# Planning around shared PSUM banks, a new order for the last triple, and last stores on two queues

## The chip, the cores and the metric

The kernel runs on one core of a Trainium2 chip. The metric is the device time of one execution in microseconds (us). Each kernel is run several times and the median counts. One further execution is recorded by the hardware profiler, and all rows and traces come from that one.

The core's engines have short names in the profile: PE is TensorE's matmul, PEld its weight load, DVE is VectorE, ACT is ScalarE, POOL is GpSimd, and SP is SyncE. A "q" behind a name (SPq) means that engine's instruction sequencer, which also issues DMAs.

## The reference

```python
# x [16, 512, 1024], w1 [1024, 768], w2 [1024, 768], all float32
y1 = np.matmul(x, w1)
y2 = np.matmul(x, w2)
return (np.tanh(y1) * y2).astype(np.float32)
```

## The kernel before

**Tiling.** The 16 x 512 rows of x are 64 row tiles of 128 rows. The columns of the two weights are put into three blocks of 512: `a` (the first 512 of w1), `b` (the first 512 of w2) and `g` (the last 256 of w1 and the last 256 of w2). K = 1024 is split into two halves of 512. All matmuls are float16 with float32 sums in PSUM, whose eight banks hold 128 x 512 each.

**Head and triples.** The first four row tiles (the head) are multiplied plainly: eight matmuls for each block. The other 60 row tiles are done in 20 triples, numbered 0 to 19. A triple is three row tiles of two halves each, times three column blocks of two halves each. Done plainly it would take 18 block products; a fast scheme needs 15, p0 to p14. Each product multiplies a sum of x blocks (`A_SUMS`, made for every triple by VectorE at L417, written S10, S21, ...) with a sum of weight blocks (`B_SUMS`, made once). A product is four matmuls of 128x128 by 128x512 (L442) and accumulates in a PSUM bank called a chain, c0 to c10.

**Between the products** stand the steps of `C_OPS`: `copy` (ScalarE, L446, bank to SBUF), `seed` (ScalarE, L446, bank to a second bank in which a later product goes on accumulating), `add` (VectorE, L452, a bank plus or minus a copy). At the end each row tile gets `t` and `th` (tanh on ScalarE, L455, 512 and 256 columns) and `m` and `mh` (the multiplication on VectorE, L460), and its output is stored (`store`, L423). A step is written with its triple: add60.19 is the step add60 of triple 19. The steps that matter below are these:

- add60 reads the bank of p0 (and a copy) and seeds the bank of p4; t0 also reads the bank of p0.
- copy60 reads the result of p4; add52 needs copy60 and the result of p5; seed16 copies add52's result and so starts the bank of p2; p3 goes on in add52's bank after seed16 has read it.
- add4 and th1 both read the result of p3; th0 reads add4's result; t1 reads add8's result, and add8 needs copy60. m1 multiplies with the result of p2, mh1 with that of p3, mh0 with add4's.
- add64 is needed by p12, add312 by p9, add2 by p5.
- The triple's third row tile has t2 and m2 (result of p13), th2 and mh2 (result of p14).

**Fillers.** Row tile 3 of the head leaves out its `g` block. Its 16 matmuls of 256 columns (L426, written m3y0k and m3y1k) are set between the products of the last triple. Then follow thg3 (tanh, L429) and mug3 (multiplication, L433).

**The order of the work.** All steps are handed to a `Planner`, which runs a small model of the engines and fixes each engine's program order. PE's order of products is written out by hand (`PE_ORDER`, and `LAST_ORDER` at L71 for triple 19) and kept strictly. For the other engines, `run` (L135) looks at each engine's ready steps: `pick` (L125) prefers, among those that can start within 0.02 us of the earliest, the one with the nearest due time. Of the engines, the one whose pick starts first goes next. A step may start when what it needs is done. The model knows nothing of two engines reading one bank at the same time: it plans t0.19 and add60.19 for the same moment. The framework that builds the program then adds the waits that keep two engines off one bank, in the planned order.

**Stores.** SyncE issues all stores. In the last triple each row tile is stored in two parts: st610, st620, st630 are the 512-column parts of row tiles 61 to 63 (multiplied by m0, m1, m2), st611, st621, st631 the 256-column parts (mh0, mh1, mh2). st3M is the last 256 columns of row tile 3, behind mug3.

**Beside it** ScalarE runs one abs instruction per row tile (D4 to D63, L386), whose sums decide at the very end, through a flag read by all engines and an `If`, whether a general path must run. For this input it does not. At the join behind the `If`, SyncE waits on several semaphores and then on all of them before the program ends.

Of the kernel before, what the change touches and what calls it, by code (L numbers as in the profile page):

```python
# [67 lines left out]

PE_ORDER = "7 0+ 13+ 6 10 4+ 5+ 9 12 1 14 3+ 2+ 11 8"
FIRST_ORDER = "7 1 10 6 12 9 11 8 14"  # L70
LAST_ORDER = "0 14 4 5 13 3 2"  # L71


class Planner:
# [9 lines left out]
    def op(self, name, engines, due, needs, fn, *args, behind=(), issued=(), chains=(), xfer=0.0, latency=None, seeds=False,  # L84
           lands=None, hold=0.0):
        assert name not in self.ops, name
        self.ops[name] = dict(engines=engines, due=due, needs=[n for n in needs if n], behind=[n for n in behind if n], issued=[n for n in issued if n], fn=fn, args=args,
                              chains=chains, xfer=xfer, latency=latency, seeds=seeds, lands=lands, hold=hold)
        for c in chains:
            self.chains.setdefault(c, {"left": 0, "bank": None, "end": 0.0})["left"] += 1  # L90

    def backward(self, margin):
        users = {n: [] for n in self.ops}
# [41 lines left out]
    def run(self):  # L135
        free = {"pe": 0.0, "act": 0.0, "dve": 0.0, "pool": 0.0, "sp": 0.0}
        bandwidth = 1.25
        left = {n: len(o["needs"] + o["behind"] + o["issued"]) for n, o in self.ops.items()}
        ready_at, end, engine_of, start_of = {n: o["hold"] for n, o in self.ops.items()}, {}, {}, {}
        ready = {e: [] for e in free}  # L140

        def release(n):
            for e in self.ops[n]["engines"]:
                ready[e].append(n)

        for n in self.ops:
            if not left[n]:
                release(n)
        position, lag = 0, 0.0
        strict = set(self.strict)  # L150
        while len(end) < len(self.ops):
            best = None
            for e, names in ready.items():
                options = []
                for n in names:
                    if n in strict and n != self.strict[position]:
                        continue
                    o = self.ops[n]
                    s = max(free[e], ready_at[n])
                    new = [c for c in o["chains"] if self.chains[c]["bank"] is None]  # L160
                    if new:
                        fit = self.fitting(o)
                        if not fit:
                            continue
                        s = max(s, min(fit)[0])
                    options.append((s, o["due"], n))
                if not options:
                    continue
                s, due, n = self.pick(e, options, lag)
                if best is None or s < best[0]:  # L170
                    best = s, e, n
            assert best, ("stuck", [(n, self.ops[n]["needs"]) for n in self.strict[position:position + 3]])
            s, e, n = best
            o = self.ops[n]
            for c in o["chains"]:
                if self.chains[c]["bank"] is None:
                    entry = min(self.fitting(o), key=lambda b: (b[0] > s, b[1] not in self.partial, b[0]))
                    self.bank_free.remove(entry)
                    self.chains[c]["bank"] = entry[1]
                    if not o["seeds"]:  # L180
                        (self.partial.add if c[0] in ("T", "f") else self.partial.discard)(entry[1])
            f = s + o["engines"][e]
            free[e] = f
            if o["lands"]:
                done = o["lands"]
                bandwidth = max(bandwidth, done - 1.6)
            elif o["xfer"]:
                bandwidth = max(bandwidth, f) + o["xfer"]
                done = bandwidth + (o["latency"] or self.LATENCY["cast" if e == "pool" else "sp"])
            else:  # L190
                done = f
            end[n], engine_of[n], start_of[n] = done, e, s
            for k in o["engines"]:
                ready[k].remove(n)
            if n in strict:
                position += 1
                lag = s - o["due"]
            for c in o["chains"]:
                chain = self.chains[c]
                chain["end"] = max(chain["end"], done + self.LATENCY[e])  # L200
                chain["left"] -= 1
                if not chain["left"]:
                    self.bank_free.append((chain["end"], chain["bank"]))
            for u in self.next.get(n, ()):
                ready_at[u] = max(ready_at[u], f)
                left[u] -= 1
                if not left[u]:
                    release(u)
            for u in self.users[n]:
                same = e in ("act", "dve", "pe") and e in self.ops[u]["engines"]  # L210
                slack = 1.0 if n in self.ops[u]["behind"] and self.ops[u]["xfer"] else 0.0
                ready_at[u] = max(ready_at[u], done + slack + (0.06 if same else 0.05 if o["xfer"] or o["lands"] else self.LATENCY[e]))
                left[u] -= 1
                if not left[u]:
                    release(u)
        self.end, self.engine_of, self.start_of = end, engine_of, start_of
        return sorted(self.ops, key=lambda n: start_of[n])
# [22 lines left out]
def kernel(  # L240
# [7 lines left out]
    nc = tc.nc  # L248
    P = 128
    B, M, K = x.shape  # L250
    _, N = w1.shape
# [6 lines left out]
    TRIPLES = (MT - HEAD) // 3  # L258
# [10 lines left out]
    of = out.flatten_outer_dims().rearrange("(mt p) n -> mt p n", p=P)  # L269
# [41 lines left out]
    pin = tc.keep_in_program_order  # L311
    engine = {"dve": nc.vector, "act": nc.scalar, "pool": nc.gpsimd, "sp": nc.sync}
    plan = Planner(8)
    op = plan.op
# [104 lines left out]
    def out_tile(mt):  # L419
        return o_bufs[mt if mt < HEAD else HEAD + (mt - HEAD) % O_BUFS]  # L420

    def store(e, mt, lo=0, n=N):
        pin(nc.sync.dma_start(of[mt][:, lo:lo + n], out_tile(mt)[:, lo:lo + n]))  # L423

    def mm(e, chain, mt, k, rhs, first):
        pin(nc.tensor.matmul(bank(chain)[:, :rhs.shape[-1]], xt(mt)[:, k, :], rhs, start=first, stop=k == KO - 1, skip_group_check=True))  # L426
# [88 lines left out]
    for n, what in enumerate(on_sp):  # L515
# [3 lines left out]
        else:  # L519
            s, k = what[0], int(what[1])  # L520
# [54 lines left out]
    outs = {mt: [] for mt in range(MT)}  # L575
# [15 lines left out]
    for n, s in enumerate("agb"):  # L591
        for mt in range(HEAD):
            if (s, mt) == ("g", HEAD - 1):
                continue
            due, behind = (lambda n: landed[slices["agb".index(s) * KO + n]] + 0.8 + 0.02 * mt), [FILL[mt]] if s == "b" and mt in FILL else []
            finals(mt, s, due(KO - 1) + (5.0, 3.0, 7.0)["agb".index(s)], plain(mt, s, due, behind))

    mt = HEAD - 1
    ends = {}
    for t, after in enumerate(("p0", "p2")):  # L600
        chain = ("f", f"y{t}")
        for n, k in enumerate(range(KO)):
            op(f"m{mt}y{t}{k}", {"pe": MM / 2}, 1e4 * (1 + t) + n, [f"cg{k}", f"e{mt}{k // KH}"], mm, chain, mt, k,
               wh[:, k, F + t * G:F + t * G + G], n == 0, behind=[f"m{mt}y{t}0" if n else f"{after}.{TRIPLES - 1}"], chains=[chain])
        ends[t] = [f"m{mt}y{t}{k}" for k in range(KO)]
        xt_readers[mt] += ends[t]
# [43 lines left out]
    LAST = 2.0  # L650
    TIME = {"t": 0.5, "m": 0.6, "th": 0.28, "mh": 0.33, "add": 0.6, "copy": 0.5, "seed": 0.5, "p": SLOT}
    soonest, until = {}, {}
# [4 lines left out]
    for i in range(TRIPLES):  # L657
# [10 lines left out]
        for o in C_OPS:  # L668
            name, kind, needs = o[:3]
            needs = [f"{n}.{i}" for n in needs]  # L670
            chains = sorted({(i, p) for p in o[3:6] if isinstance(p, str) and p[0] == "c"})
# [14 lines left out]
                continue  # L686
            r = o[3]
            mt = HEAD + 3 * i + r
            due = soonest[i, name] + LAST
            if kind in ("t", "th"):  # L690
                lo, n = (0, F) if kind == "t" else (F, G)
                op(f"{name}.{i}", {"act": 0.5 if n == F else 0.285}, due, needs, c_tanh, i, r, o[4], lo, n, o[5],
                   behind=reuse_out(mt), chains=chains)
            else:
                lo, n, at = (0, F, 0) if kind == "m" else (F, G, G)
                op(f"{name}.{i}", {"dve": 0.6 if n == F else 0.335}, due + 1, needs, c_mul, i, r, o[4], lo, n, at, chains=chains)
                outs[mt].insert(0 if kind == "m" else 1, f"{name}.{i}")
    for mt in range(MT):
        i = (mt - HEAD) // 3 if mt >= HEAD else -1
        if mt < HEAD:  # L700
            n = F if mt == HEAD - 1 else N
            op(f"st{mt}", {"sp": 0.05}, 1e3, outs[mt][:1] if mt == HEAD - 1 else outs[mt], store, mt, 0, n, behind=[f"p12.{4 + mt}"], xfer=1.0)
            if n < N:
                op(f"st{mt}M", {"sp": 0.05}, 2e4, outs[mt][1:], store, mt, n, N - n, xfer=0.4)
            continue
        late = [f"{('p0', 'p4', 'p12')[(mt - HEAD) % 3]}.{i + 1}"] if i < TRIPLES - 2 else []
        if i == TRIPLES - 1:
            for a, lo, n in ((0, 0, F), (1, F, G)):
                part = outs[mt][a:a + 1]
                op(f"st{mt}{a}", {"sp": 0.05}, 2e4, part, store, mt, lo, n, xfer=0.4)  # L710
        else:
            op(f"st{mt}", {"sp": 0.05}, slot_of[max(i, 0), "p2"] + 12, outs[mt], store, mt, behind=late, xfer=1.0)
    for mt in range(BY_PE, MT):
# [9 lines left out]
    for mt in range(HEAD, MT):  # L723
        i, r = divmod(mt - HEAD, 3)
# [16 lines left out]
    for n in sorted(soon, key=lambda n: plan.start_of[n]):  # L741
        o = plan.ops[n]
# [3 lines left out]
    for n in order:  # L746
        if n not in soon:
            o = plan.ops[n]
# [102 lines left out]
```

## Time and profile before

| what | us |
|---|---|
| three runs | 302.2, 301.41, 301.7 |
| median | 301.7 |
| the profiled execution | 301.63 |
| its span, first to last instruction | 299.9 |
| PE busy in it | 291.0 |
| DVE busy | 255.9 |
| ACT busy | 224.9 |

The granted TensorE clock of the profiled execution is 0.999 of full speed. The span is what the trace shows; the profiled execution took 1.73 us more than it. A busy PE means that matmuls are in flight, not that they follow each other at the best rate; idle time of an engine counts only where the last work waits for it. The chain of waits follows the work that ended last back from the end, and so names what each stretch of the span waited for. In rows of the timeline, `[0.52 <-ACT o L455]` means that the engine stood idle for 0.52 us and was released by ScalarE's instruction of line 455 that writes `o`.

### The profile page before, as it was taken

To read this page: it belongs to the slowest core of one execution; us is meant where nothing else is said; L and a number is where in the kernel's file an instruction comes from. 1 tells how busy PE (TensorE), PEld (TensorE's weight loads), DVE (VectorE), ACT (ScalarE), POOL (GpSimd) and SP (SyncE) were. 2 spreads that over 40 slices of the span, in tenths; PEclk is the share of its full clock that TensorE was granted. 3 is DMA by queue.
4 is the path that set the end of the run, shared out by engine and by line. 5 is a ranking of instruction groups with operands and counts; after the bars stand their busy time and mean duration, and the time that the engine had idled before them with its cause. 6 is when DMAs were issued, how large, how long until landed. Compare 5 with 4: busy or idle time off the path is not lost.

```text
span 299.9 us, 4690 instructions
## 1 busy us (share of the span) xinstructions
PE 291.0 (97%) x1385; PEld 133.8 (45%) x1385; DVE 255.9 (85%) x538; ACT 224.9 (75%) x451; POOL 49.8 (17%) x128
## 2 busy tenths in 40 slices
PE   8989999999999999999999999999999999999994
PEld 5434444444444444444444444444444444444442
DVE  1669989989889898988988898898988989897874
ACT  2587997597978879798786988759687776867542
POOL 0064042121102102211011211112022110000000
PEclk9999999999999999999999999999999999999999
DMA  6999999999999999999999999999999999141233
GB/s 231 380 291 200 178 184 169 176 223 237 244 168 187 229 173 301 272 254 259 161 243 243 300 204 258 221 245 252 190 224 251 145 224 296 56 160 52 106 143 142
DMA packets 84283, 63.51 MB, mean 212 GB/s; under 512 B 62752, under 2 KB 66336, under 8 KB 84256
## 3 DMA queue, kind: packets, MB, share of 16 engines
q1 hardware_dynamic: 73888, 45.36, 61.9%
q0 software_dynamic: 9792, 16.78, 37.6%
q10 hardware_dynamic: 576, 1.05, 1.0%
q8 instruction: 11, 0.18, 0.2%
q14 instruction: 16, 0.13, 0.2%
HBM read 39.85 MB, written 25.17 MB: 217 GB/s over the span
## 4 chain that ended last, share of the span: by engine, by line
PE 85%; DMA 7%; DVE 4%; issue 1%; ACT 1%; ACTq 0%; SPq 0%; POOL 0%; DVEq 0%
PE bank L442 82%; DMA arena<-in_w_dram 4%; PE bank L426 3%; DMA wh<-in_w_dram 2%; DMA xT<-xh 1%; DVE bank L452 1%; DVE early_x L417 1%; DVE o L460 1%; PE bank L376 0%; DVE arena L452 0%; ACTq L353 0%; DVE b L408 0%; ACT o L455 0%; ACT wh L362 0%; SPq L350 0%
## 5 line engine op out<-in xcount | busy, mean ns | idle before, releaser
L442 PE MATMUL bank<-b,early_x 128*128 128x512 f16 x640 | 148.2, 379 | 0.8 <-DVE bank L452 0.4
L442 PEld LDWEIGHTS <-early_x 128*128 128x128 f16 x800 | 78.2, 98 | 95.7 <-issue 1.7
L446 ACT ACTIVATE arena<-bank 128x512 f32<-128x512 f32 x100 | 59.0, 597 | 38.8 <-PE bank L442 37.9
L452 DVE TENSOR_TENSOR bank<-bank,arena 128x512 f32<-128x512 f32 x100 | 69.3, 694 | 19.0 <-ACT arena L446 13.6
L460 DVE TENSOR_TENSOR o<-o,bank 128x512 f32<-128x512 f32 (+1 forms) x120 | 61.1, 548 | 5.2 <-ACT o L455 3.5
L386 ACT ACTIVATE junk<-xh 128x1024 f16<-128x1024 f16 x60 | 63.1, 1051 | 0.1
L442 PEld LDWEIGHTS <-xT 128*128 128x128 f16 x400 | 38.9, 98 | 47.9 <-issue 1.2
L442 PE MATMUL bank<-b,xT 128*128 128x512 f16 x240 | 58.3, 379 | 0.0
L358 POOL DMA_DIRECT2D xh<-in_x_dram x60 | 31.8, 530 | 77.6 <-ACT junk L386 60.2
L442 PE MATMUL bank<-wh,xT 128*128 128x512 f16 x160 | 41.1, 379 | 0.8 <-DVE o L460 0.5
L455 ACT ACTIVATE o<-bank 128x256 f32<-128x256 f32 (+1 forms) x80 | 32.9, 436 | 11.2 <-DVE bank L452 7.7
L442 PE MATMUL bank<-wh,early_x 128*128 128x512 f16 x160 | 41.1, 379 | 0.0
L417 DVE TENSOR_TENSOR early_x<-early_x,xT 128x512 f16<-128x512 f16 x80 | 32.2, 418 | 1.3 <-DMA xT<-xh 0.6
L455 ACT ACTIVATE o<-arena 128x512 f32<-128x512 f32 x40 | 25.0, 624 | 6.8 <-DVE arena L452 6.7
L479 POOL CAST held<-xT 128x1 f32<-128x1 f16 x53 | 12.6, 239 | 103.7 <-DMA xT<-xh 103.7
L446 ACT ACTIVATE bank<-bank 128x512 f32<-128x512 f32 x40 | 21.5, 570 | 1.6 <-DVE bank L452 1.1
L426 PE MATMUL bank<-wh,xT 128*128 128x512 f16 x72 | 19.1, 379 | 1.4 <-DVE wh L364 0.7
L417 DVE TENSOR_TENSOR early_x<-xT,early_x 128x512 f16<-128x512 f16 x40 | 16.7, 418 | 0.0
L417 DVE TENSOR_TENSOR early_x<-xT,xT 128x512 f16<-128x512 f16 x40 | 16.6, 416 | 0.0
L452 DVE TENSOR_TENSOR bank<-arena,bank 128x512 f32<-128x512 f32 x20 | 13.9, 695 | 2.4 <-PE bank L442 0.5
L452 DVE TENSOR_TENSOR arena<-arena,bank 128x512 f32<-128x512 f32 x20 | 13.5, 677 | 0.3 <-issue 0.3
L452 DVE TENSOR_TENSOR arena<-bank,arena 128x512 f32<-128x512 f32 x20 | 13.8, 688 | 0.0
(47 smaller groups left out, 136.0 us busy)
## 6 DMA issues: line engine op xcount, KB each, us to landing
out_dram<-o SPq DMA_DIRECT2D x60, 384.0 KB, 5.5
xh<-in_x_dram POOLq DMA_DIRECT2D x60, 256.0 KB, 6.3
arena<-in_w_dram SPq DMA_DIRECT2D x12, 256.0 KB, 5.7
early_x<-in_x_dram SPq DMA_DIRECT2D x8, 256.0 KB, 5.4
arena<-in_w_dram ACTq DMA_DIRECT2D x4, 256.0 KB, 6.1
wh<-in_w_dram POOLq DMA_DIRECT2D x8, 128.0 KB, 4.9
out_dram<-o SPq DMA_DIRECT2D x4, 256.0 KB, 2.7
xT<-xh SPq DMA_TRANSPOSE x57, 6.1
```

The costliest lines, as they stand in the source:

```text
L358: pin(nc.gpsimd.dma_start(xh(mt), xf[mt]))
L386: pin(nc.scalar.activation(junk[:, :src.shape[-1]], src, ACT.Abs, scale=scale, accum_out=sums[:, column:column + 1]))
L417: pin(engine[e].tensor_tensor(x_operand(i, v), x_operand(i, a), x_operand(i, b), OP[how]))
L426: pin(nc.tensor.matmul(bank(chain)[:, :rhs.shape[-1]], xt(mt)[:, k, :], rhs, start=first, stop=k == KO - 1, skip_group_check=True))
L442: pin(nc.tensor.matmul(place(i, dst), x_operand(i, a)[:, k, :], w_rhs(b, k), start=begins and k == 0, stop=k == KH - 1, skip_group_check=T ...
L446: pin(nc.scalar.activation(place(i, dst), place(i, src), ACT.Copy, scale=float(sign)))
L452: pin(nc.vector.tensor_tensor(place(i, dst), a, b, ALU.add if signs == (1, 1) else ALU.subtract))
L455: pin(nc.scalar.activation(out_tile(HEAD + 3 * i + r)[:, lo:lo + n], place(i, src)[:, :n], ACT.Tanh, scale=float(sign)))
L460: pin(nc.vector.tensor_tensor(o, o, place(i, src)[:, at:at + n], ALU.mult))
L479: pin(nc.gpsimd.tensor_copy(held, xt(mt)[:, 0, :1]))
```

## The change

The planner now notes for each chain when ScalarE and when VectorE last finished on it. A step of one of them may only be planned after the other's last one on the same chain, plus that engine's latency. Of two engines whose picks start at the same time, the one with the nearer due time goes first.

`LAST_ORDER` changes, and both groups of fillers may start once p14.19 is planned (before: the first group after p0.19, the second after p2.19). Their matmuls keep a late due time and fill what the products leave. th1.19 is due 1.0 us later.

The last stores (st3M, and all parts of triple 19) may be issued by SyncE or by ScalarE, at 0.4 us in the plan.

```diff
-LAST_ORDER = "0 14 4 5 13 3 2"
+LAST_ORDER = "0 5 4 13 14 3 2"
+FILLERS = "p14", "p14"
...
-            self.chains.setdefault(c, {"left": 0, "bank": None, "end": 0.0})["left"] += 1
+            self.chains.setdefault(c, {"left": 0, "bank": None, "end": 0.0, "act": 0.0, "dve": 0.0})["left"] += 1
...
+                    if e in ("act", "dve"):
+                        other = "dve" if e == "act" else "act"
+                        s = max([s] + [self.chains[c][other] + self.LATENCY[other] for c in o["chains"]])
                     options.append((s, o["due"], n))
...
-                if best is None or s < best[0]:
-                    best = s, e, n
+                if best is None or (s, due) < best[0]:
+                    best = (s, due), e, n
...
-            s, e, n = best
+            (s, _), e, n = best
...
                 chain["end"] = max(chain["end"], done + self.LATENCY[e])
+                if e in ("act", "dve"):
+                    chain[e] = done
...
     def store(e, mt, lo=0, n=N):
-        pin(nc.sync.dma_start(of[mt][:, lo:lo + n], out_tile(mt)[:, lo:lo + n]))
+        pin(engine[e].dma_start(of[mt][:, lo:lo + n], out_tile(mt)[:, lo:lo + n]))
...
-    for t, after in enumerate(("p0", "p2")):
+    for t, after in enumerate(FILLERS):
...
-            due = soonest[i, name] + LAST
+            due = soonest[i, name] + LAST + (1.0 if (i, name) == (TRIPLES - 1, "th1") else 0.0)
...
-                op(f"st{mt}M", {"sp": 0.05}, 2e4, outs[mt][1:], store, mt, n, N - n, xfer=0.4)
+                op(f"st{mt}M", {"sp": 0.4, "act": 0.4}, 2e4, outs[mt][1:], store, mt, n, N - n, xfer=0.4)
...
-                op(f"st{mt}{a}", {"sp": 0.05}, 2e4, part, store, mt, lo, n, xfer=0.4)
+                op(f"st{mt}{a}", {"sp": 0.4, "act": 0.4}, 2e4, part, store, mt, lo, n, xfer=0.4)
```

In the program that this builds, PE's order in triple 19 is p0, p5, p4, p13, p14, four fillers, p3, p2, twelve fillers; before it was p0, p14, one filler, p4, p5, p13, seven fillers, p3, p2, eight fillers. On ScalarE st631 stands between t1.19 and th0.19, and st621 and st3M behind thg3. SyncE keeps st610, st630, st620 and st611, in this order. VectorE's last steps are add4, m1, mh1, mh0, mug3; before they were add4, mh1, m1, mh0, mug3. ScalarE's order there is th0, th1, thg3; before it was thg3, th1, th0.

## The prediction

> **What bounds the kernel now.** I read the page first. Its first part says which engine is full.
>
> ```profile
> span 299.9 us, 4690 instructions
> ...
> PE 291.0 (97%) x1385; PEld 133.8 (45%) x1385; DVE 255.9 (85%) x538; ACT 224.9 (75%) x451; POOL 49.8 (17%) x128
> ```
>
> PE is busy 97% of the span, so only time in which PE waits, or time after its last matmul, can be won. Next the chain of waits in order of time (start, length, what) shows where that is.
>
> ```profile
> 54.43 223.86 PE bank L442 x1036
> ...
> 278.31 9.53 PE bank L442 x44
> ...
> 287.86 0.61 ACT o L455
> ...
> 288.49 0.71 DVE bank L452
> ...
> 289.24 2.75 PE bank L442 x12
> ...
> 293.67 0.71 DVE bank L452
> ...
> 294.40 0.39 ACT o L455
> ...
> 296.09 0.41 DVE o L433
> ```
>
> From 54.43 to 287.8 the chain is PE alone: 223.86 / 1036 = 0.216 us per 512-wide matmul, so a product of four takes 0.86. Then it leaves PE twice: for t0.19 and add60.19 (287.86 to 289.20), and after p3.19 for add4.19, th1.19 and the last multiplications. The timeline of the first place:
>
> ```profile
> 286.80 1.03 PE L442 MATMUL bank<-b,xT 128*128 128x512 f16 x4
> ...
> 287.86 0.60 ACT L455 ACTIVATE o<-bank 128x512 f32<-128x512 f32 x1
> ...
> 288.49 0.70 DVE L452 TENSOR_TENSOR bank<-bank,arena 128x512 f32<-128x512 f32 x1 [0.52 <-ACT o L455]
> ...
> 289.24 0.59 PE L442 MATMUL bank<-b,early_x 128*128 128x512 f16 x2 [0.45 <-DVE bank L452]
> 289.25 0.31 PEld L442 LDWEIGHTS <-early_x 128*128 128x128 f16 x2 [0.62 <-issue]
> ```
>
> p0.19 starts at 286.80 and its readers at 287.86, so a product's result is there 1.06 after its first matmul. t0.19 (ScalarE) and add60.19 (VectorE) both only read its bank, yet add60.19 starts 0.03 after t0.19 ends: the two are kept apart on a bank. p4.19 needs add60.19. Without a wait it would have followed p14.19 (287.66 + 0.86) and one filler (0.11), at 288.63; it starts at 289.24, so 0.61 is lost. Last, the end, from the SyncE rows of the store line and of the join after the last `If`:
>
> ```profile
> L423 SPq DMA_DIRECT2D out_dram<-o x9: 332/333/1670, 286.2 to 296.8; - x9
> ...
> L753 SPq EVENT_SEMAPHORE  x5: 17/17/17, 297.3 to 297.6; - x5
> ...
> L846 SPq EVENT_SEMAPHORE  x14: 17/28/28, 298.2 to 299.8; - x14
> ```
>
> The last multiplication ends at 296.50, the last store is issued at 296.76 and lands 1.9 later, at 298.63. Behind the issue SyncE runs five waits 0.08 apart from 297.31, then the final waits; the one for the last store passes at 298.73, 0.06 after its neighbour like the rest, so no wait holds it. The end is SyncE's own work behind its last issue.
>
> **The change, part by part**, on the clock of the trace before.
>
> *The loop.* In the built order, PE's first difference is behind p0.19, and POOL has none. VectorE and ScalarE exchange neighbours in triples 0, 1, 4, 9 and 18: D22 ahead of t0.4, D37 ahead of t0.9, add8 ahead of add52, and the like. Some banks swap numbers, which costs nothing. SyncE gets one transpose (T28) ahead of two stores, whose out tiles are reused nine row tiles later. What covers this is the lead of the feeds: seed16 ends 1.0 before p3 in nearly every triple, and 0.47 in triple 9, 0.33 in triple 18; add64.5 ends 1.62 before p12.5, add64.10 1.03 before p12.10. add52 goes back by one VectorE step (0.60), but seed16 starts 0.6 to 0.7 after add52 in triples 4 and 9, behind ScalarE work. t0.4 goes back by an abs instruction (1.05 plus 0.2 for its sum); add60 no longer waits for it, and the m0 behind it leaves add64 inside the lead. In triple 18 copy60 moves ahead of t2.19 and starts some 1.0 earlier than its 281.09, which pays for add8 ahead of add52. Without the cover a place would cost 0.1 to 0.6; I take nothing, and the head (before 54) stays: its stall at 53.56 hangs on mh1.0, which does not move.
>
> *Last triple, order of PE.* p0, p5, p4, p13, p14, four fillers, p3, p2, twelve fillers. p5.19 takes p14's place at 287.66; it needs add2.19, which ends at 287.66 (0.05 at worst). add60.19 now stands ahead of t0.19: 287.87 to 288.57. p4.19 starts at 288.62 against 289.24: 0.62 won. t0.19 goes behind (288.60 to 289.20), and only m0.19 waits for it. p13 and p14 (0.86 each) and four fillers (0.44) bring PE to 291.64. Meanwhile: p4's result 289.68, copy60.19 0.60, add52.19 0.70, seed16.19 0.60, with 0.03 to 0.05 at each handover: p3.19 at 291.69, against 292.60. Here 0.91 is won, because add52.19 stood until 291.24 for p5.19, which is now done early.
>
> *The end of compute.* p2.19 starts at 292.55, its result is there at 293.61, and m1.19 now goes directly behind add4.19: 293.61 to 294.31 (before: 295.15 to 295.84). Before, VectorE stood 0.45 for th1.19, which had waited for add4.19 on the same bank; now m1.19 fills that time. PE's last filler ends at 293.41 + 12 x 0.11 + 0.16 = 294.9, so mug3 runs from 294.93 to 295.34 against 296.50: 1.16 won.
>
> *The stores.* st631, st621 and st3M move to ScalarE's queue. Behind st631 stand th0.19, th1.19 and thg3: it waits for mh2.19 (done about 292.6) and takes 0.33 to 0.46 (the store rows, and the ScalarE loads of the first microseconds). th0.19 waits for add4.19 until 293.4 anyway, so this is covered by some 0.3; uncovered it would move thg3 and mug3 by as much. The other two have no compute behind them. Before, SyncE's four last issues queued, so that st3M began 0.26 after mug3 instead of the usual 0.03: 0.23 is what a second queue can give. The Trainium skill says the same in "DMA: Bandwidth & Descriptors", section "Issuing engines are not separate DMA queues": starting transfers on several engines saves only the sequencer's time. By it alone the move would be worth those 0.23 and no landing would change.
>
> *What is late next.* SyncE's last issue (st611, behind mh0.19) ends near 295.4, so its own tail would start 1.7 earlier. But in the built program the second of the five waits counts the store of m1.19 (st620). That is issued at 294.34 and, with the 2.0 of the equal store before, lands at 296.36; the wait passed at 297.39 before. So everything behind it moves by 1.0. st3M, issued at 295.37 and landing after 1.9, is there at 297.3; its final wait comes 1.34 behind the second one, at 297.7, and is not held.
>
> **Sum.** 1.0 off the span: 298.9. The profiled execution took 301.63, 1.73 more than its span, so 300.6; it lies 0.07 under the median of 301.7. Forecast 300.7.
>
> **Rivals.**
> 1. *More is won.* If SyncE's join wait is not held (a store that lands in 1.7, as the smaller ones do, gives 0.3 of it), the last store sets the end: landing at 297.3 against 298.7 for its wait, 1.4 won, 300.3. For it: landings of 1.7 occur. Against it: the 512-wide halves took 2.0.
> 2. *The cover is lost.* The chain p4, copy60, add52, seed16 ends at 291.64, exactly when PE arrives with only four fillers instead of seven before p3. One VectorE or ScalarE instruction in its way (0.4 to 0.6) passes straight to m1 and st620: 0.4 to 0.6 won, 301.1 to 301.3. For it: no slack. Against it: m0.19 ends near 289.9, 0.4 before add52 is wanted.
> 3. *ScalarE's queue lands late: slower.* The only rows of that queue are the first loads:
>
> ```profile
> arena<-in_w_dram ACTq DMA_DIRECT2D x4, 256.0 KB, 6.1
> ...
> out_dram<-o SPq DMA_DIRECT2D x4, 128.0 KB, 1.9
> ```
>
> If st3M took 6.1 from 295.37, it would land at 301.5 and the end come 1.2 later, at 302.6: 2.7 lost, 304.4. It decides from a landing of 3.4, where the end is as before. Against it: SyncE's equal loads in the same crowd took 5.7, and at the end the DMA engines are nearly idle; but one SyncE issue there took 1.67 instead of 0.33. By the rule above (Trainium skill, "DMA: Bandwidth & Descriptors", "Issuing engines are not separate DMA queues") this rival has nothing for it, since the queues share their engines.
>
> That the change does not do what it says is excluded for the order (the built program shows it), not for its worth.
>
> **How the numbers follow.** A measurement of this kernel tells 0.3% (0.9 us) from no change. Forecast 0.50, rival 1 0.17, rival 2 0.23, rival 3 0.10. The forecast lies just past that bound, so I put two thirds of it (0.33) to faster; with rival 1 that makes 0.50. Same: 0.17 of the forecast, rival 2's 0.23, and 0.02 of rival 3: 0.42. Slower: 0.08. The range runs from rival 1 less 0.2 (300.1) to rival 2 plus 0.4 (301.7), about the scatter of the three runs (301.41 to 302.2).
>
> **What would show it.** Right: p4.19 starts within 0.15 of the end of p5.19, PE idles under 0.1 before p3.19, VectorE has no wait for ScalarE behind add4.19, mug3 ends 8.5 after p0.19 starts, against 9.70, and SyncE's second join wait stands for a landing. Wrong: a new idle piece of PE between 54 and 287, a wait of PE on ScalarE before p3.19, or a final wait held by a ScalarE store.

## The result, and the profile after

The changed kernel takes 300.03 us (median of 22 runs) against 301.44 for the kernel before (22 runs beside it). The ratio is 0.9958, with a 95% interval of 0.9945 to 0.9970: faster by 0.4%, just past the 0.3% that can be told. Applied to the 301.7 from which the prediction started, that is 300.4 (300.0 to 300.8); 300.7 was forecast. The profiled execution took 299.76, its span is 297.9.

The page's first part shows the same picture as before, one percent fuller:

```profile
span 297.9 us, 4694 instructions
...
PE 290.5 (98%) x1385; PEld 134.1 (45%) x1385; DVE 256.0 (86%) x538; ACT 224.8 (75%) x451; POOL 51.6 (17%) x128
```

The chain of waits on this page holds only mug3 (0.42 us), so it answers nothing. A table by stage does. Below it is first for the kernel before, then for the changed one. The cuts are the starts of p7.1, p7.2 and p0.19; columns are the stretch, its length, then busy time and instructions of each engine, the clock, the DMA share and GB/s.

```profile
core 0: us, PE busy (x) PEld busy (x) DVE busy (x) ACT busy (x) POOL busy (x), PEclk, DMA share, GB/s
0.00:40.77 40.77, 37.37 (x205) 18.62 (x205) 27.92 (x63) 28.17 (x52) 10.68 (x26) 1.00 1.05 250
40.77:54.43 13.66, 13.16 (x60) 5.81 (x61) 13.49 (x31) 11.54 (x25) 4.01 (x11) 1.00 1.11 161
54.43:286.80 232.37, 232.37 (x1078) 105.20 (x1079) 207.50 (x433) 180.60 (x366) 35.12 (x92) 1.00 1.03 211
286.80:299.86 13.06, 8.12 (x45) 4.20 (x43) 6.95 (x14) 4.60 (x10) 0.00 (x0) 0.98 0.44 163
```

```profile
0.00:40.31 40.31, 36.95 (x204) 18.79 (x205) 28.07 (x64) 27.74 (x52) 10.52 (x26) 1.00 1.06 255
40.31:53.48 13.17, 13.12 (x61) 5.81 (x60) 13.17 (x30) 11.65 (x25) 5.91 (x13) 1.00 1.03 192
53.48:285.74 232.26, 232.26 (x1078) 105.31 (x1078) 207.70 (x434) 181.03 (x367) 35.21 (x91) 1.00 0.99 209
285.74:297.89 12.15, 8.14 (x45) 4.20 (x43) 7.05 (x13) 4.43 (x10) 0.00 (x0) 0.93 0.47 175
```

The last stage is 0.91 shorter: that is the forecast term (1.0 was forecast). But the second stage is 0.49 shorter, the loop 0.11, and the first 0.46. The forecast had nothing for these three. In the second stage VectorE is busy 13.49 of 13.66 us before and 13.17 of 13.17 after: it has no idle time at all there.

The first place of triple 19, as the timeline of the changed kernel shows it (start, length, engine and operation, idle time before it and its releaser):

```profile
286.60 2.05 PE L448 MATMUL bank<-b,early_x 128*128 128x512 f16 x8
...
286.87 0.70 DVE L458 TENSOR_TENSOR bank<-bank,arena 128x512 f32<-128x512 f32 x1
287.61 0.60 ACT L461 ACTIVATE o<-bank 128x512 f32<-128x512 f32 x1 [1.07 <-DVE bank L458]
287.63 1.39 PEld L448 LDWEIGHTS <-early_x 128*128 128x128 f16 x7 [0.28 <-issue]
288.24 0.69 DVE L466 TENSOR_TENSOR o<-o,bank 128x512 f32<-128x512 f32 x1 [0.67 <-ACT o L461]
```

add60.19 runs first. ScalarE is idle for 1.07 ahead of t0.19, and the last 0.7 of it is add60.19. p4.19 starts at 287.63, behind p5.19 with 0.16 of idle time inside the row of eight matmuls (before: 0.61). The end of the work:

```profile
290.21 0.60 PE L432 MATMUL bank<-wh,xT_kept 128*128 128x256 f16 x4
...
290.68 1.89 PE L448 MATMUL bank<-b,xT 128*128 128x512 f16 x8
...
291.74 0.69 DVE L458 TENSOR_TENSOR bank<-arena,bank 128x512 f32<-128x512 f32 x1 [0.21 <-PE bank L448]
...
292.66 1.35 DVE L466 TENSOR_TENSOR o<-o,bank 128x512 f32<-128x512 f32 x3 [0.23 <-PE bank L448]
...
293.71 1.06 ACTq L429 DMA_DIRECT2D out_dram<-o  x2
293.99 0.42 DVE L439 TENSOR_TENSOR o<-o,bank 128x256 f32<-128x256 f32 x1
```

p3.19 starts 0.14 after the last of the four fillers, where fillers follow each other by 0.11: 0.03 is lost. VectorE waits for PE only, no longer for ScalarE. Last the stores and the join: the rows of the two lines (count, shortest, median and longest in ns, first and last start), and from SyncE's waits the one behind the join.

```profile
L429 ACTq DMA_DIRECT2D out_dram<-o x3: 338/350/362, 291.6 to 294.4; - x3
...
L759 SPq EVENT_SEMAPHORE  x5: 17/17/17, 294.5 to 295.7; - x5
...
L852 SPq EVENT_SEMAPHORE  x14: 17/28/28, 296.2 to 297.8; - x14
```

```profile
SPq L429 <- DVE o L466: 4.5, 3, 2.2
SPq L759 <- SPq L759: 0.9, 1, 0.9
```

The five join waits spread from 294.5 to 295.7, because the second stands 0.9. It counts m1.19's store st620, issued at 293.38, which landed at 295.41; the wait passed at 295.43.

### The profile page after: what moved, and what is told of

It is laid out like the page before. It is cut to its first block, busy times and chain, and to the rows that moved or that the text cites. A ratio compares the mean times of both kernels' runs of the same rounds, so it can differ in the third digit from the quotient of the medians.

```text
span 297.9 us, 4694 instructions
## 1 busy us (share of the span) xinstructions
PE 290.5 (98%) x1385; PEld 134.1 (45%) x1385; DVE 256.0 (86%) x538; ACT 224.8 (75%) x451; POOL 51.6 (17%) x128
## 5 line engine op out<-in xcount | busy, mean ns | idle before, releaser
L485 POOL CAST held<-xT 128x1 f32<-128x1 f16 x53 | 14.9, 282 | 35.1 <-DMA xT<-xh 35.1
```

The lines of the kernel that those rows point to most:

```text
L485: pin(nc.gpsimd.tensor_copy(held, xt(mt)[:, 0, :1]))
```

## The experiments

All lengths below are from the profiles, cut as in the table above; "ratio" is against the runs of the kernel before on the same chip.

| kernel | ratio (95%) | to p7.1 | p7.1 to p7.2 | p7.2 to p0.19 | p0.19 to end |
|---|---|---|---|---|---|
| before | | 40.77 | 13.66 | 232.37 | 13.06 |
| changed | 0.9958 (0.9945 to 0.9970) | 40.31 | 13.17 | 232.26 | 12.15 |
| changed, again (e11) | 0.9967 (0.9945 to 0.9990) | 40.73 | 13.41 | 232.26 | 12.14 |
| e1 order only | 0.9991 (0.9979 to 1.0002) | 40.45 | 13.67 | 232.38 | 12.73 |
| e2 rule only | 0.9960 (0.9945 to 0.9975) | 42.58 | 13.41 | 232.26 | 12.53 |
| e3 stores only | 0.9999 (0.9990 to 1.0008) | 40.36 | 13.66 | 232.38 | 13.08 |
| e4 order and rule | 0.9970 (0.9948 to 0.9993) | 40.96 | 13.42 | 232.25 | 12.14 |
| e5 order and stores | 0.9993 (0.9977 to 1.0009) | 40.27 | 13.66 | 232.36 | 12.72 |
| e6 rule and stores | 0.9973 (0.9961 to 0.9985) | 40.46 | 13.40 | 232.25 | 12.56 |
| e7 whole store | 0.9959 (0.9945 to 0.9972) | 40.60 | 13.34 | 232.26 | 12.31 |
| e8 order, one exchange | 0.9960 (0.9945 to 0.9975) | 40.59 | 13.67 | 232.37 | 12.18 |
| e9 one exchange, triple 0 | 0.9997 (0.9988 to 1.0006) | 40.76 | 13.42 | 232.38 | 13.05 |
| e10 changed, mh1.0 earlier | 0.9936 (0.9922 to 0.9951) | 40.55 | 12.96 | 232.26 | 12.13 |
| e12 before, mh1.0 earlier | 0.9984 (0.9971 to 0.9998) | 41.15 | 13.01 | 232.38 | 13.06 |

The first column scatters from 40.27 to 42.58 with no relation to the edits, so the 0.46 of the first profile there is scatter (e11 has 0.04). The other three repeat to 0.1 between kernels with the same edits, with one exception that is taken up under e11.

**e1, the order alone:** `LAST_ORDER`, `FILLERS` and th1.19's due time.

```diff
-LAST_ORDER = "0 14 4 5 13 3 2"
+LAST_ORDER = "0 5 4 13 14 3 2"
+FILLERS = "p14", "p14"
...
```

> Only the new order of PE's last triple and of the fillers (and th1.19's later due time); planner and stores as before. Theory A (the win is p4.19 no longer waiting for t0.19, which only the planner's rule brings): add60.19 still starts after t0.19 ends, p4.19 starts 2.4 to 2.5 us after p0.19 (before 2.44, changed kernel 1.89) with only p5.19 to cover it, so PE idles about 0.7 there; p3.19 comes 0.3 earlier, and from the start of p0.19 to the end of the span it takes 12.7 to 12.8 us (before 13.10, changed kernel 12.16). Time 0.3 to 0.4 us less than before. Theory B (the order of PE alone brings the win): 12.2 us from p0.19 to the end, 0.9 us less than before. Theory C (the planner's rule wins in the first triples): p7.2 starts where it does before (54.4), not 1 us earlier.

p4.19 starts 2.44 after p0.19, as before, p3.19 at 5.50 (before 5.81), the end comes at 12.73. The order alone gives 0.33 of the end and nothing elsewhere: theory A.

**e2, the rule alone:** the planner's lines.

```diff
+                    if e in ("act", "dve"):
+                        other = "dve" if e == "act" else "act"
+                        s = max([s] + [self.chains[c][other] + self.LATENCY[other] for c in o["chains"]])
...
-                if best is None or s < best[0]:
+                if best is None or (s, due) < best[0]:
...
```

> Only the planner's rule (ScalarE and VectorE apart on a bank, nearer due time first); order of PE and stores as before. Theory A: add60.19 starts with p0.19's result, p4.19 1.83 to 1.90 us after p0.19, and from p0.19 to the end 12.3 to 12.4 us (13.10 before): the second join wait of SyncE stands for the store of m1.19. Time 0.7 to 0.8 us less. Theory B: little is won, because p3.19 waits for seed16.19 as before: 12.9 or more. Theory C: p7.2 starts 0.5 to 1 us earlier than before, as in the changed kernel (53.5 against 54.4), and the time falls by 1.2 us or more.

p4.19 at 1.88, p3.19 at 5.25, the end at 12.53: 0.53 of the end. Theory A expected 12.3 to 12.4, with a join wait held for the store of m1.19. That did not come: the five join waits run 0.08 apart, and SyncE's own sequence behind its last issue sets the end. The second stage is 0.25 shorter, not 0.5 to 1 as theory C had it, and the loop 0.11. In the median of the runs the rule is most of the gain. It has two parts (the two engines apart on a bank, and the nearer due time first); which of them brings which exchange was not tried.

**e4, order and rule, with SyncE issuing every store.**

```diff
-        pin(engine[e].dma_start(of[mt][:, lo:lo + n], out_tile(mt)[:, lo:lo + n]))
+        pin(nc.sync.dma_start(of[mt][:, lo:lo + n], out_tile(mt)[:, lo:lo + n]))
...
```

> The changed kernel with all last stores on SyncE. Theory A (the end hangs on the landing of m1.19's store, for which the join waits, not on who issues): from p0.19 to the end 12.1 to 12.3 us as in the changed kernel (12.16), time the same as the changed kernel's within 0.1 us. Rival (the second queue gives its issue time or more): 0.23 us or more slower than the changed kernel, 12.4 or more. Theory C: p7.2 starts at 53.5 as in the changed kernel.

The end comes at 12.14, as in the changed kernel. SyncE's last issue starts at 9.03 instead of 8.30, its five join waits run from 9.59 to 9.91 without a hold; with ScalarE's help they start at 8.79 and the last passes at 9.93. What the second queue saves there, the wait for st620's landing takes back. Theory C, p7.2 at 53.5, did not come: the second stage is 13.42 (see e11).

**e8, the order, and add60.19 ahead of t0.19 by hand, no rule.**

```diff
...
-                   behind=reuse_out(mt), chains=chains)
+                   behind=reuse_out(mt), chains=chains, hold=285.9 if (i, name) == (TRIPLES - 1, "t0") else 0.0)
```

> As the kernel with the order alone, but t0.19 is planned 0.2 us later, so that add60.19 stands ahead of it: of all that the planner's rule does, this one exchange. Theory A: p4.19 starts 1.83 to 1.90 us after p0.19, p3.19 4.9 to 5.0 after it; VectorE's end is 0.15 later than in the changed kernel (mh1 before m1, with th1 waiting for add4), but the join wait is not held, so from p0.19 to the end it takes 12.0 to 12.2 us: the whole win of the tail. Time 0.9 to 1.0 us less than before. Rival (the rest of the rule, th1 behind m1, matters too): 12.5 us or more. Theory C: p7.2 at 54.4 as before, and so this kernel is slower than the changed kernel by the part won in the first triples.

p4.19 at 1.89, p3.19 at 4.94, the end at 12.18, and the second stage 13.67 as before. So at the end the rule is this one exchange. (A gain of 0.9 in 301.3 would be a ratio of 0.997. The one measured, from six runs, is lower, but 0.997 lies inside its interval.)

**e3, the stores alone.**

```diff
...
-                op(f"st{mt}{a}", {"sp": 0.05}, 2e4, part, store, mt, lo, n, xfer=0.4)
+                op(f"st{mt}{a}", {"sp": 0.4, "act": 0.4}, 2e4, part, store, mt, lo, n, xfer=0.4)
```

> The kernel before, with its last stores on SyncE or ScalarE and nothing else of the change. SyncE issues st631, st630, st611, ScalarE st610, st621, st620, st3M. Theory A (a second queue shortens SyncE's own tail but moves no landing): PE's order and its stalls stay (p4.19 starts 2.44 after p0.19, p3.19 at 5.8, a stall of 0.61 ahead of p4.19), mug3 ends at 9.70; the last store, st3M behind mug3, lands 1.9 to 2.1 after an issue at 9.75, so the end comes 12.6 to 12.9 after the start of p0.19 (before 13.1): 0.2 to 0.5 us less, 300.8 to 301.1. Rival B (ScalarE's strict queue: st610 stands ahead of copy60.19 and waits for m0.19): copy60.19 and p3.19 move back by 0.3 or more, the end is at 13.1 or later, the time 301.3 to 301.8.

Neither: PE's work is where it was (p3.19 at 5.81, mug3 done at 9.70), and the end is at 13.08. The last join wait passes at 10.44 instead of 10.83, but then a final wait is held. From SyncE's waits:

```profile
SPq L846 <- DMA out_dram<-o: 0.4, 1, 0.4
SPq L753 <- SPq L753: 0.3, 1, 0.3
```

st3M, issued 0.23 earlier, landed some 2.2 after its issue instead of 1.9. The kernel before had SyncE's own tail and this landing 0.1 apart, so shortening one showed the other.

**e6, rule and stores, old order.** The diffs of e2 and e3 together.

> The planner's rule and the stores on two queues, without the new order of triple 19. Theory A (the rule is worth 0.2 to 0.45 in the head and 0.5 to 0.6 in triple 19 through add60.19 ahead of t0.19; the stores are worth nothing or 0.2): p4.19 starts 1.9 after p0.19, p3.19 at 5.25, PE's stall ahead of p7.2 is 0.2 to 0.46, the end comes 12.3 to 12.55 after p0.19, time 300.3 to 300.7. Rival B (the rule's gain was in the end that SyncE sets, and the stores give more once ScalarE carries half of them): end at 12.0 or sooner, 300.0. Rival C (st631 and the issues ahead of th0.19 delay mug3): end at 12.6 or later, 300.9.

12.56 against 12.53 in e2, which is 0.01 past theory A's range; second stage and loop are as in e2. So the stores are worth nothing here either: the join starts sooner, but its second wait then stands 0.6 for a landing.

**e7, the changed kernel with row tile 62 stored whole,** so that the join counts only stores that landed long before.

```diff
+        if i == TRIPLES - 1 and mt == HEAD + 3 * i + 1:
+            op(f"st{mt}", {"sp": 0.4}, 2e4, outs[mt], store, mt, xfer=0.4)
...
```

> The changed kernel, but row tile 62 is stored whole, in one DMA of 768 columns (384 KB) behind m1.19 and mh1.19, in place of st620 and st621. SyncE's five join waits then count only stores that landed long before. Theory A (in the changed kernel the second join wait stands 0.9 for the landing of st620, and this sets the end): the five waits run 0.08 apart without a hold, the end is set by the landing of the last stores, 11.8 to 12.0 after the start of p0.19 (changed kernel 12.15), 0.15 to 0.35 us less than the changed kernel, 299.8. Rival B (a wait for the last store's landing stands right behind, so that the hold is only moved): end at 12.1 to 12.2, same time. Rival C (a store of 384 KB lands later than two parts, by 0.3 or more): end at 12.3 or later.

The join waits run from 9.18 to 9.50 with no hold, 0.43 sooner than in the changed kernel, which shows that the hold there was st620's landing. But the end comes at 12.31, 0.16 later. That is the number of rival C, but not its mechanism: the whole store itself landed 2.32 after its issue, and no wait stood for it. The waits of SyncE say where the time went:

```profile
SPq L854 <- DMA out_dram<-o: 0.6, 2, 0.4
```

Two final waits stand for the last two 128-KB stores, which landed 2.4 after their issue (2.1 in the changed kernel), beside one of 384 KB. That the large store slowed them is likely, but no run shows it by itself.

**e9, the kernel before with add60.0 behind S31.1 and add2.0.** VectorE alone; the place is in triple 0.

```diff
-                    op(f"{name}.{i}", {"dve": 0.6}, None, needs, c_add, i, *o[3:], behind=before, chains=chains, seeds=True)
+                    op(f"{name}.{i}", {"dve": 0.6}, None, needs, c_add, i, *o[3:], behind=before, chains=chains, seeds=True,
+                       hold=42.2 if (i, name) == (0, "add60") else 0.0)
```

> The kernel before with one exchange on VectorE: add60.0 stands behind S31.1 and add2.0 and no longer ahead of them; no other engine's order changes, and triple 19 stays as it was. Theory A (VectorE stands idle in triple 0 behind mh2.0 until t0.0 is through with the bank that add60.0 reads, and since VectorE is full until mh1.0 this idle time reaches p7.2): PE's stall ahead of p7.2 falls from 0.66 to 0.4, p7.2 starts 13.4 after p7.1 (before 13.66), the last triple stays at 13.1, time 0.25 us less than before, 301.1. Rival B (the shorter stall comes from triple 1's exchange or from elsewhere): stall stays at 0.66, p7.2 at 13.66 after p7.1, time as before. Rival C (add60.0 later makes p4.0 wait): a new stall in triple 0, time 0.1 to 0.3 more.

The second stage falls to 13.42, what every kernel with the rule has, and nothing else moves. The ratio (0.9997) can't tell the 0.24 from nothing; the profile can. VectorE's timeline in the kernel before, then in e9:

```profile
42.76 0.41 DVE L460 TENSOR_TENSOR o<-o,bank 128x256 f32<-128x256 f32 x1
43.34 0.70 DVE L452 TENSOR_TENSOR bank<-bank,arena 128x512 f32<-128x512 f32 x1 [0.17 <-ACT o L455]
43.94 0.41 DVE L417 TENSOR_TENSOR early_x<-xT,early_x 128x512 f16<-128x512 f16 x1
```

```profile
42.74 0.41 DVE L460 TENSOR_TENSOR o<-o,bank 128x256 f32<-128x256 f32 x1
43.08 0.42 DVE L417 TENSOR_TENSOR early_x<-xT,early_x 128x512 f16<-128x512 f16 x1
43.41 1.29 DVE L452 TENSOR_TENSOR bank<-bank,arena 128x512 f32<-128x512 f32 x2
```

Before, add60.0 stood for t0.0 on its bank, the same pair as in triple 19. From the start of mh2.0 to that of the next step it took 0.58, in e9 0.34. VectorE then has no idle time up to mh1.0, ten microseconds later, so the 0.24 arrives there whole. PE's wait behind mh1.0 shrinks by 0.21, and another stall of PE, of 0.05 near 47.7, is gone. PE's row at p7.2, in the kernel before and then in e9:

```profile
54.43 1.02 PE L442 MATMUL bank<-wh,xT 128*128 128x512 f16 x4 [0.50 <-DVE o L460]
```

```profile
54.18 1.02 PE L442 MATMUL bank<-wh,xT 128*128 128x512 f16 x4 [0.29 <-DVE o L460]
```

**e10, the changed kernel with mh1.0 ahead of S15.2 and add128.1.** If VectorE's full queue is the cause, moving mh1.0 forward in it must remove the rest of the stall. p7.2 keeps its planned time, so that nothing else is planned anew.

```diff
...
+                   hold=52.3666 if (i, name) == (2, "p7") else 0.0)
...
-                op(f"{name}.{i}", {"dve": 0.6 if n == F else 0.335}, due + 1, needs, c_mul, i, r, o[4], lo, n, at, chains=chains)
+                op(f"{name}.{i}", {"dve": 0.6 if n == F else 0.335}, due if (i, name) == (0, "mh1") else due + 1, needs, c_mul, i, r, o[4], lo, n, at, chains=chains)
```

> The changed kernel, with mh1.0 moved on VectorE ahead of S15.2 and add128.1 (0.41 + 0.69 us of work); nothing else moves on any engine. Theory A (p7.2 waits for the bank that mh1.0 reads, and mh1.0 only for its place in VectorE's full queue): PE's stall ahead of p7.2 is gone (0.22 to 0.46 in the kernels with the rule), p7.2 starts 12.95 to 13.0 after p7.1, add128.1 still ends 1.8 before p13.1; the time is 0.2 to 0.45 less than the changed kernel's, 299.7 to 299.9. Rival B (p7.2 waits for something else too, m1.0 or a landing): stall stays above 0.2, time as the changed kernel. Rival C (the work moved back makes another product late): a new stall between 53 and 60, time the same or more.

The stage by windows:

```profile
40.55:53.51 12.96, 12.96 (x62) 5.85 (x61) 12.96 (x30) 11.46 (x24) 5.88 (x11) 1.00 1.09 199
```

PE is now busy for all of it, 12.96 = 15 products of 0.86. The time is 299.33 against 300.24 for the changed kernel on the same chip. The profiles explain 0.45 of these 0.9; the ratios' intervals (0.9922 to 0.9951 and 0.9945 to 0.9990) allow that and more, and what the rest is, if it is real, stays open. It is the fastest version here (six runs), below both kernels.

**e11, the changed kernel again.**

> The changed kernel once more, as the base for the others of this call and as a second profile. If the 0.22 ahead of p7.2 in its first profile was lower than the 0.45 of the other kernels with the rule because p7.1 began without a wait for its transposed tile, the second profile shows 0.45 where that wait is there and 0.2 where it is not; p7.2 starts 13.2 to 13.4 after p7.1. The last triple repeats to 0.05: p4.19 1.89, p3.19 4.94, the end 12.15 after p0.19; a second join wait held for the store of m1.19 by 0.9.

The second stage is 13.41 and the stall 0.45, as in e2, e4 and e6; the end repeats to 0.01. The reason expected for the first profile's 0.22 falls: e6 has no wait ahead of p7.1 and still 0.45. What the traces show is that S11.1 on VectorE started 1.13 before p7.1 in that profile and 0.90 in e11, where VectorE had first stood idle for 0.40 until a transposed tile landed (39.83 in e11's timeline; no idle time there in the first profile). Each VectorE step up to mh1.0 keeps these 0.24. The second stage of the change is thus worth 0.25 and, by chance of the execution, 0.49.

**e5, order and stores without the rule.** The diffs of e1 and e3 together.

> The changed kernel without the planner's rule: the new order of triple 19 and the stores on two queues. Theory A (the rule is what puts add60.19 ahead of t0.19 in triple 19 and shortens the stall ahead of p7.2; the stores are worth nothing): p4.19 2.44, p3.19 5.50, the end 12.6 to 12.75 after p0.19, PE's stall ahead of p7.2 0.66; time 0.3 to 0.45 less than before, 300.9 to 301.0. Rival B (stores and order need each other): the end at 12.3 or sooner, 300.6 or less. Rival C (st610 ahead of copy60.19 on ScalarE waits and delays p3.19): p3.19 at 5.8 or later, time as before.

The end comes at 12.72, as e1's 12.73, and the second stage takes 13.66, as before: theory A.

**e12, the kernel before with mh1.0 ahead of mh2.1, S15.2 and add128.1.** The edit of e10 in the kernel before.

> The kernel before, with mh1.0 moved on VectorE ahead of mh2.1, S15.2 and add128.1; nothing else moves, the last triple and its stores stay. Theory A (the stall ahead of p7.2 is VectorE's full queue ahead of mh1.0 and nothing else): the stall of 0.66 is gone, p7.2 starts 12.95 to 13.0 after p7.1 (13.66 before), the end stays 13.1 after p0.19; time 0.6 to 0.7 less than before, a ratio of 0.998: as much as the order of triple 19 alone gave or more. Rival B (without the rule another step, add4.0 or m1.0, is late as well): the stall falls to 0.2 to 0.45 only, time 0.2 to 0.45 less. Rival C (time won in the head is lost again in the loop, where landings pace PE): p0.19 starts as in the kernel before, 246.03 after p7.1, time as before.

p7.2 starts 13.01 after p7.1, without a stall, and p0.19 245.39 after p7.1 instead of 246.03: the 0.64 is kept through the loop, which refutes rival C. The ratio, 0.9984 (0.9971 to 0.9998), holds the 0.64 (0.9979) as well as 0.1.

## Why the prediction was right, and where not

**The last triple: right.** Every step came as forecast, and a little smaller. p4.19 was forecast 0.62 earlier against p0.19 and came 0.56 earlier, p3.19 0.91 and 0.87, the end of m1.19 1.53 and 1.42, that of mug3 1.16 and 1.03. PE's stall ahead of p4.19 is 0.16, a little over the 0.15 named as the bound. Order and exchange are both needed: 0.33 by the order (e1), 0.53 by the rule (e2), 0.92 together (e4).

**The end: right, also in its mechanism.** "The second of the five waits counts the store of m1.19": it did, stood 0.9, and passed 0.02 after the landing, 2.04 behind the issue. The forecast was 1.0 off the span, and 0.91 to 0.92 came. It is not the only limit there: in e8 the join is not held, and the end is at 12.18.

**The stores: right.** They were to give at most 0.23 and gave nothing (e3 is 0.02 longer at the end, e4 and the changed kernel differ by 0.01, e5 and e6 from the same kernels without the second queue by 0.03 at most). What was not seen is why nothing at all: close behind SyncE's own sequence stands another limit each time, a final wait for the last landing in e3 (held 0.4) and st620's landing in the changed kernel (held 0.9). ScalarE's last two stores landed after 2.1, with an issue of 0.34 to 0.36 against SyncE's 0.33. That settles rival 3. It fits the rule of the Trainium skill in "DMA: Bandwidth & Descriptors", "Issuing engines are not separate DMA queues", that starting transfers on several engines saves only the sequencer's time. One argument against rival 3 was wrong, though: the DMA engines are not nearly idle at the end, their busy share in the last stage is 0.44 before and 0.47 after.

**Rivals 1 and 2: refuted.** The join was held, and where it is not (e7) the last landing sets the end at 12.31, so the 1.4 of rival 1 was not there to be had. Against rival 2, PE lost only 0.03 ahead of p3.19 in the changed kernel, although that place has no slack.

**The head and the loop: wrong.** The step that failed is "the head (before 54) stays: its stall at 53.56 hangs on mh1.0, which does not move". mh1.0 kept its place among its neighbours, but the exchange in triple 0, which the same paragraph names, took 0.24 of idle time out of the queue ahead of it, ten microseconds earlier (e9). The order of instructions had been compared, not the time that passed in them; the busy time of VectorE in this stretch, 13.49 of 13.66, would have shown that a wait there has nowhere to be made up. For the loop "I take nothing" stood. The cover held, as no kernel with the rule has a new stall of PE there, but 0.11 came on top. All kernels without the rule have a PE stall of 0.10 to 0.12 near 171, and none with it; in the kernel before, p7.11 starts there 0.05 after VectorE's m1.9 ends (171.03). Which exchange removed it was not tried.

So the span of the change by its parts: 0.92 at the end, 0.25 at p7.2, 0.11 in the loop, together 1.28; e11's profiled execution is 1.31 under that of the kernel before (301.63 - 300.32), and the medians of its runs and those beside it differ by 1.24. The 22 runs of the result differ by 1.41; the intervals allow both. Of the 1.28 the rule gives 0.53 + 0.25 + 0.11 = 0.89, the order the rest. The forecast of 1.0 stood for the end alone, and its size was right there. That it also came near the whole is partly luck: the end gave 0.08 less than forecast, and head and loop gave 0.36 that nobody had forecast.

## What to carry to other kernels

Where a queue is full for a long stretch, look for idle time on it as far back as the last gap, not at the neighbours of the late step: in e9 an early wait of 0.24 was delivered whole at the other end. When two engines read one bank, write the order by who is needed next; a planner that does not know of the conflict leaves it to chance at every such place. Here that order was worth 0.53 at the end (e2) and 0.24 in the head (e9). Before moving the last issues to a second queue, see how far the next limit is: here it was 0.1 us away.

## What the runs showed of the hardware

The last three 128-KB stores landed 1.7 to 2.2 us after their issue, from either engine (kernel before, changed kernel, e3). The differences are as large as what a sooner issue could save: 2.1 for all three in the changed kernel, 2.4 for the last two of e7, beside a store of 384 KB. From the last of the five join waits to the end of the span it is 2.22 to 2.23 us wherever no final wait is held (before, changed, e4, e6), so the end of this kernel is set more than 2 us ahead of it.
